# Placing the first feed-forward units' transfers and the modulation columns in a two-layer hybrid trunk

## The chip, the cores and the metric

One core of a Trainium2 chip. The metric is the device time of one execution in microseconds (us); a kernel's time is the median of its runs. Five engines run their own instruction queues in order: TensorE (PE, with its weight loads as PEld), VectorE (DVE), ScalarE (ACT), GpSimd (POOL) and SyncE (SP). SP, ACT and POOL also issue DMA transfers from their queues.

## The reference

Two layers of a decoder trunk over a sequence of 1024 positions with 1024 channels. Each layer has a mixer (scan, pooling and attention side by side, then one output projection) and a gated feed-forward part of width 2816 with a causal convolution of width 3. Both are modulated by a vector that is computed from the condition `c`:

```python
c_act = jax.nn.silu(c)
for i in range(DEPTH):
    mod = (c_act @ ada_w[i] + ada_b[i])[:, None, :]
    sh1, sc1, g1, sh2, sc2, g2 = jnp.split(mod, 6, axis=-1)
    h = rmsnorm(x, norm1_g[i]) * (1.0 + sc1) + sh1
    ...
    x = x + g1 * (mix @ w_out[i])
    h = rmsnorm(x, norm2_g[i]) * (1.0 + sc2) + sh2
    x = x + g2 * conv_ffn(h, ffn_up[i], ffn_conv_w[i], ffn_conv_b[i], ffn_down[i])
return rmsnorm(x, final_g)

def conv_ffn(h, up, conv_w, conv_b, down):
    hid = causal_dwconv(h @ up, conv_w, conv_b)
    g, u = jnp.split(hid, 2, axis=-1)
    return (jax.nn.silu(g) * u) @ down
```

## The kernel before, in words

Activations lie with 128 channels on the partitions and the 1024 positions along the row, so `x` is eight tiles of 128x1024; `H0` and `H1` are the two halves of a row. A 32-bit product is made of three matmuls: both operands are split into a rounded part (`whi`, an ACT cast) and a rest (`wlo`, a DVE subtraction).

**Order.** The program is written as a sequence of tile operations. A scheduler sets the order on each engine: it takes operations by priority (their place in the code) as soon as their tiles and dependencies allow it, so an operation whose inputs are free early is placed far ahead of its line. `after(ins, dep, info)` (line 78) adds a dependency by hand. With `nosync`, the default, it only holds the order; with `sync` the instruction also waits for `dep` on the chip.

**End of the output projection.** The projection has two groups of four input chunks. The second group is `accum_last` (line 1233), called at line 1148. It goes over the first half of the positions for eight output tiles `n`, and then over the second half. Per tile: load the weights through `wraw` (line 265, two raw buffers, issued on SP) and split them, 12 matmuls into a bank `dn`, add into `x[n]` on DVE (`accum`, line 1210), store `x[n]` to memory from ACT's queue (`store`, line 893), square on ACT and add the square into `acc` (`square_add`, line 182: POOL for `n` up to 6, DVE for the last). The weights of tiles 4 to 7 are kept for the second half (`wkeep`). After a half, `rstd_begin` (line 198) sums `acc` over the partitions on PE (`ssps`, L203), ACT and DVE make the scale from it, and `rstd_spread` (line 208) spreads it on PE (L211). Through the second half run `first_half` (line 896), which makes the operands `B` of the first half, and at its end `begin` (line 994), the first seven products of the up projection. `second_half` starts `others` (line 912), which makes the operands T1 to T4 and B22; its subtractions `xx` at L918 run on POOL.

**Up projection.** Pairs of columns are made as 22 units, each with seven products instead of eight, on sums of weight blocks: `S1`, `S2`, `S3`, `S4`, and the plain blocks `A11`, `A12`, `A22`. `prepare` (line 1018) loads the blocks: plain transfers on SP (`up_w`, line 987) and adding transfers on POOL's queue (`plus`): S1 and S3 from memory, then S1 into S2, then S2 into S4. The blocks lie in a ring of sixteen 128x512 buffers. For units 0 and 1 `prepare` is called ahead of `accum_last` (lines 1146 and 1147). Their plain transfers wait for the last accumulation of the first group (`group_last`), and their eight adding transfers are put in the list `pending`. `sums` (line 1010), called per tile, hands them out in the second half; but the scheduler holds no order between them and the tile, so it places them on POOL where their blocks are loaded.

**Modulation columns.** `ada_col` (line 138) makes one column of the modulation: two transfers of 256 KB on SP (`araw`) and two DVE products with a sum. In layer 0's up projection twelve columns are written, one behind each unit from 7 to 18 (`ada`, line 1152). They use the two raw buffers of `wraw`. `finish` (line 1172) does the convolution of a unit, its silu, the product `fg<-fg,fu` on DVE and the store `act_d` on SP.

Of the kernel before, what the change touches and what calls it, by code (L numbers as in the profile page):

```python
# [12 lines left out]
ALU = mybir.AluOpType  # L13
# [41 lines left out]
def tile_trunk(ctx, tc, xT_d, c_d, ck_d, adas_d, pos_d, par_d, pff_d, fg_d, adaw_d, win_d, wv_d, poolw_d, wout_d, up_d, down2_d, down_d,  # L55
               cmask_d, crow_d, out_d):
    nc = tc.nc
# [76 lines left out]
    x = []  # L134
    act.activation(ccol, ccol, AF.Silu)
    act.activation(cact, cact, AF.Silu)

    def ada_col(l, j, take=None):

        for i in range(2):  # L140
            r = take("araw") if take else rawp.tile([128, 528], F32, tag="raw", name="araw")[:, 0:512]
            nc.sync.dma_start(r, adaw_d[l, j, :, HALF[i]])
            dve.scalar_tensor_tensor(r, r, 1.0, cact[:, HALF[i]], ALU.mult, ALU.mult,  # L143
                                     accum_out=mod[l][:, j:j + 1] if i == 0 else mod2[:, j % 8:j % 8 + 1])
        if j % 8 == 7:
            s = slice(j - 7, j + 1)
            dve.tensor_tensor(mod[l][:, s], mod[l][:, s], mod2, op=ALU.add)
            ada_fin(l, j // 8, 0, 8)
# [33 lines left out]
    def square_add(acc, t, first, eng=dve):  # L182
        if first:
            return act.activation(acc, t, AF.Square)
        sq = p2("sq", "nh", 3)[:, 0:acc.shape[-1]]
        r = act.activation(sq, t, AF.Square)
        eng.tensor_tensor(acc, acc, sq, op=ALU.add)  # L187
        return r

    def rstd(acc, n, tab):  # L190
# [20 lines left out]
            spread_last[0] = mm(ps[:, b * 128:(b + 1) * 128], r[:, b:b + 1].to_broadcast([128, 128]), ident, start=True, stop=True)  # L211
        return ps[:, 0:nb * 128]

    spread_last = [None]

    def modulate(l, which, k, hs, rs, hi, lo):
        t = p2("ht", "nh", 3)[:, 0:rs.shape[-1]]
# [651 lines left out]
    def ffn(l, ys, end):  # L869
# [135 lines left out]
                    units[f].V1 = pb("pv", ("ps", "ps", "po")[f])  # L1005
                    product(units[f].V1, raw, "B21", True, spread_last[0] if i == 3 else None, w)

        pending = []

        def sums(part, n):  # L1010

            if part and pending and n < 7:
                pending.pop(0)()
                if n == 6:
                    while pending:
                        pending.pop(0)()

        def prepare(f):

            u = units.setdefault(f, Unit())  # L1020
            dep = group_last[0] if f < 2 else None

            def plus(t, src):
                add = lambda: nc.gpsimd.dma_start(t, src, accum_op=ALU.add)  # L1024
                if f < 2:
                    pending.append(add)
                else:
                    add()

            if f > 3:  # L1030
                u.A11 = up_w("A11", f, 0)
            u.S1 = up_w("S1", NFF + f, 0, dep)
            u.S2 = up_w("S2", f, 0, dep)
            u.S3 = up_w("S3", f, 0, dep)
            plus(u.S1, up_d[l, NFF + f, :, HALF[1]])
            plus(u.S3, up_d[l, NFF + f, :, HALF[0]])
            plus(u.S2, u.S1)
            u.A22 = up_w("A22", NFF + f, 1, dep)
            if f > 2:
                u.A12 = up_w("A12", f, 1)  # L1040
            u.S4 = up_w("S4", f, 1, dep)
            plus(u.S4, u.S2)
# [100 lines left out]

        minus = pff[:, 0:132].rearrange("p (s c) -> p s c", s=3)[:, :, NFF:2 * NFF]
        dve.tensor_scalar(minus, minus, -1.0, None, op0=ALU.mult)
        prepare(0)
        prepare(1)
        accum_last(wout_d[l, 1], ys, 16, l, None, PARTS[0], first_half, begin, second_half, store, sums)

        todo = [(0, 40 + k) for k in range(8)] + [(1, p * 8 + k) for p in (1, 0, 2, 4, 3, 5) for k in range(8)] if l == 0 else []  # L1150

        def ada(n, take=None):
            for _ in range(n):
                if todo:
                    ada_col(*todo.pop(0), take)

        def acts(fs, pool):
            out = []
# [8 lines left out]
            return out  # L1167


        si = None  # L1170

        def finish(f):
            nonlocal si
            p = units.pop(f)
            g = conv(p.G, f, "fg")
            u = conv(p.U, NFF + f, "fu")
            si = act.activation(g, g, AF.Silu)
            dve.tensor_tensor(g, g, u, op=ALU.mult)
            (nc.sync if f < NFF - 2 else nc.gpsimd).dma_start(act_d[f], g)

        for f in range(NFF + 1):
# [26 lines left out]
    cnt_, group_last = [0], [None]  # L1208

    def accum(ps, n, hs, gcol, l):  # L1210
        dve.scalar_tensor_tensor(x[n][:, hs], ps, mod[l][:, gcol + n:gcol + n + 1], x[n][:, hs],
                                 ALU.mult, ALU.add)

    def acc_ps():
# [18 lines left out]
    def accum_last(src, m, gcol, l, dep, parts, then, early, rest=None, store=None, sums=None):  # L1233

        mh, ml = zip(*m)
        tab = table(dep)
        w, done = [], None
        for hs in parts:
            acc = p2("acc", "nr", 2)[:, 0:hs.stop - hs.start]
            for n in range(8):  # L1240
                if not done:
                    w.append(wquad(src, n, True))
                elif early:
                    then(n, *done)
                ps = acc_ps()[:, 0:hs.stop - hs.start]
                gemm(ps, w[n], mh, ml, hs, range(4))
                accum(ps, n, hs, gcol, l)
                if store:
                    store(n, hs)
                square_add(acc, x[n][:, hs], n == 0, nc.gpsimd if rest and n < 7 else dve)  # L1250
                if sums:
                    sums(hs.start, n)
                if done and not early:
                    then(n, *done)
            done = hs, rstd_spread(*rstd_begin(acc, D, "pt", tab))
        if early:
            early()
        if rest:
            rest(*done)
        else:  # L1260
            for n in range(8):
                then(n, *done)
# [134 lines left out]
```

## Time and profile before

| | us |
|---|---|
| median of three runs | 2290.52 |
| lowest and highest | 2285.11, 2291.4 |
| the profiled execution | 2287.57 |
| its span in the trace | 2285.8 |
| granted clock of PE over the span | 0.991 of full speed |

In a profile's row, times are us from the start of the span; L161 is line 161 of the kernel. `dn<-yh,whi` names what is written and what is read, without buffer numbers. What stands in square brackets is the idle time of the engine just before the instruction, and what ended it. In the list of waits the columns are: who waited for whom, us in total, how often, the longest. In a row by windows, each engine has its busy time with the number of instructions in brackets, and the last three numbers are PE's granted clock, the busy share of the DMA engines and GB/s. SPq, ACTq and POOLq are the queues from which an engine issues transfers.

### The profile page before, as it was taken

To read this page: it belongs to the slowest core of one execution; us is meant where nothing else is said; L and a number is where in the kernel's file an instruction comes from. 1 tells how busy PE (TensorE), PEld (TensorE's weight loads), DVE (VectorE), ACT (ScalarE), POOL (GpSimd) and SP (SyncE) were. 2 spreads that over 40 slices of the span, in tenths; PEclk is the share of its full clock that TensorE was granted. 3 is DMA by queue.
4 is the path that set the end of the run, shared out by engine and by line. 5 is a ranking of instruction groups with operands and counts; after the bars stand their busy time and mean duration, and the time that the engine had idled before them with its cause. 6 is when DMAs were issued, how large, how long until landed. Compare 5 with 4: busy or idle time off the path is not lost. (4 is left out here: it accounts for less than half of the span.)

```text
span 2285.8 us, 29760 instructions
## 1 busy us (share of the span) xinstructions
PE 2225.1 (97%) x10472; PEld 1808.7 (79%) x10472; DVE 1553.3 (68%) x2712; ACT 1057.5 (46%) x1960; POOL 243.4 (11%) x308
## 2 busy tenths in 40 slices
PE   6999999999999999999999999998999999999998
PEld 4878877778788888788888888776888888878887
DVE  6467888588766667995564567775966666675446
ACT  5366664355454445312234667533645455442212
POOL 0210000231111110000001000003211111100000
PEclk9999999999999999999999999999999999999999
DMA  7452333658876776991133221236777777663112
GB/s 275 130 146 79 93 112 126 164 161 221 212 197 172 179 175 202 338 298 59 56 134 108 56 56 48 87 106 183 181 179 174 175 175 179 162 244 106 47 47 88
DMA packets 186229, 338.94 MB, mean 148 GB/s; under 512 B 28704, under 2 KB 44320, under 8 KB 186080
## 3 DMA queue, kind: packets, MB, share of 16 engines
q1 hardware_dynamic: 126144, 244.44, 32.8%
q0 software_dynamic: 30560, 61.56, 15.0%
q10 hardware_dynamic: 29376, 31.05, 4.1%
q8 instruction: 82, 1.34, 0.2%
q14 instruction: 67, 0.55, 0.1%
HBM read 265.93 MB, written 44.83 MB: 136 GB/s over the span
## 5 line engine op out<-in xcount | busy, mean ns | idle before, releaser
L161 ACT CAST whi<-wraw 128x512 fp32r<-128x512 f32 (+2 forms) x196 | 117.6, 602 | 394.6 <-PE dq L233 274.1
L232 PE MATMUL dq<-ah,whi 128*128 128x512 f32 x576 | 227.0, 394 | 1.8 <-DVE xd L1230 1.4
L233 PE MATMUL dq<-al,whi 128*128 128x512 f32 x576 | 226.8, 394 | 0.0
L234 PE MATMUL dq<-ah,wlo 128*128 128x512 f32 x576 | 226.0, 393 | 0.0
L161 ACT CAST whi<-S 128x512 fp32r<-128x512 f32 x176 | 108.7, 619 | 206.9 <-PE px L970 129.0
L162 DVE TENSOR_TENSOR wlo<-wraw,whi 128x512 fp32r<-128x512 f32 (+2 forms) x196 | 129.8, 665 | 103.9 <-ACT whi L161 99.2
L1230 DVE SCALAR_TENSOR_TENSOR xd<-dq,mod,xd 128x1024 f32<-128x1024 f32 x80 | 102.7, 1284 | 123.8 <-PE dq L234 123.8
L162 DVE TENSOR_TENSOR wlo<-S,whi 128x512 fp32r<-128x512 f32 x176 | 124.5, 707 | 80.7 <-ACT whi L161 78.5
L143 DVE SCALAR_TENSOR_TENSOR araw<-araw,cact 128x512 f32<-128x512 f32 x160 | 106.1, 689 | 52.2 <-DMA araw<-in_adaw 51.8
L969 PE MATMUL px<-T24h,whi 128*128 128x512 f32 x352 | 138.9, 395 | 2.6 <-ACT s L1046 2.6
L971 PE MATMUL px<-T24h,wlo 128*128 128x512 f32 x352 | 138.3, 393 | 1.9 <-DVE wlo L162 1.9
L970 PE MATMUL px<-T24l,whi 128*128 128x512 f32 x352 | 138.5, 393 | 0.1
L969 PE MATMUL pv<-B,whi 128*128 128x512 f32 x344 | 135.7, 394 | 0.0
L970 PE MATMUL pv<-B,whi 128*128 128x512 f32 x344 | 135.6, 394 | 0.0
L971 PE MATMUL pv<-B,wlo 128*128 128x512 f32 x344 | 135.3, 393 | 0.0
L232 PEld LDWEIGHTS dq<-ah,whi 128*128 128x128 f32 x576 | 108.3, 188 | 28.0 <-issue 1.9
L1137 DVE SCALAR_TENSOR_TENSOR fg<-G,pff,fg 128x1023 f32<-128x1023 f32 x88 | 112.7, 1281 | 24.4 <-ACT fg L1135 24.3
L234 PEld LDWEIGHTS dq<-ah,wlo 128*128 128x128 f32 x576 | 108.4, 188 | 25.0 <-DVE wlo L162 0.5
L161 ACT CAST whi<-A 128x512 fp32r<-128x512 f32 x118 | 72.5, 615 | 118.9 <-PE pv L970 58.0
L233 PEld LDWEIGHTS dq<-al,whi 128*128 128x128 f32 x576 | 108.5, 188 | 23.9
L162 DVE TENSOR_TENSOR wlo<-A,whi 128x512 fp32r<-128x512 f32 x118 | 80.9, 686 | 63.8 <-ACT whi L161 59.5
L1024 POOL DMA_DIRECT2D S<-S x88 | 75.9, 871 | 430.2 <-DMA S<-in_up 284.2
(403 smaller groups left out, 5891.0 us busy)
## 6 DMA issues: line engine op xcount, KB each, us to landing
S<-in_up SPq DMA_DIRECT2D x176, 256.0 KB, 3.0
araw<-in_adaw SPq DMA_DIRECT2D x160, 256.0 KB, 4.2
A<-in_up SPq DMA_DIRECT2D x118, 256.0 KB, 3.6
S<-in_up POOLq DMA_DIRECT2D x88, 256.0 KB, 5.3
S<-S POOLq DMA_DIRECT2D x88, 256.0 KB, 4.0
raw<-act_d SPq DMA_DIRECT2D x88, 256.0 KB, 3.8
act_d<-fg SPq DMA_DIRECT2D x40, 512.0 KB, 3.6
wraw<-in_down SPq DMA_DIRECT2D x80, 256.0 KB, 2.7
```

Of the source, the lines that this page charges most:

```text
L143: dve.scalar_tensor_tensor(r, r, 1.0, cact[:, HALF[i]], ALU.mult, ALU.mult, accum_out=mod[l][:, j:j + 1] if i == 0 else mod2[:, j % 8:j % ...
L161: act.copy(hi[:, 0:n], raw)
L162: dve.tensor_tensor(lo[:, 0:n], raw, hi[:, 0:n].bitcast(F32), op=ALU.subtract)
L232: mm(ps, wh, hi[k][:, s], start=i == 0, stop=False)
L233: mm(ps, wh, lo[k][:, s], start=False, stop=False)
L234: mm(ps, wl, hi[k][:, s], start=False, stop=i == n - 1)
L969: after(mm(ps, wh[:, c], h_, start=first and k == 0, stop=False, skip_group_check=not first), dep)
L970: mm(ps, wh[:, c], l_, start=False, stop=False, skip_group_check=not first)
L971: mm(ps, wl[:, c], h_, start=False, stop=k == 3, skip_group_check=not first)
L1024: add = lambda: nc.gpsimd.dma_start(t, src, accum_op=ALU.add)
L1137: dve.scalar_tensor_tensor(acc[:, s:T], t[:, 0:T - s], pff[:, (2 - s) * 44 + cc:(2 - s) * 44 + cc + 1], acc[:, s:T], ALU.mult, ALU.add)
L1230: group_last[0] = dve.scalar_tensor_tensor(x[n], ps, mod[l][:, gcol + n:gcol + n + 1], x[n], ALU.mult, ALU.add)
```

## The change

Three edits. (1) `prepare` of units 0 and 1 is called from `sums` at tile 6 of the first half, and their plain transfers wait for that tile's accumulation (`row`). (2) Their adding transfers are tied in order to the adds of the squares: S1 and S3 behind tile 2 of the second half, S2 behind tile 4, S4 behind tile 6. (3) In the up projection each column's DVE products stand, in order only, behind the product of the unit finished last (`fg_last`). In the down projection (`take` given) columns have no such dependency.

```diff
-    def ada_col(l, j, take=None):
+    def ada_col(l, j, take=None, dep=None):
...
-            dve.scalar_tensor_tensor(r, r, 1.0, cact[:, HALF[i]], ALU.mult, ALU.mult,
-                                     accum_out=mod[l][:, j:j + 1] if i == 0 else mod2[:, j % 8:j % 8 + 1])
+            after(dve.scalar_tensor_tensor(r, r, 1.0, cact[:, HALF[i]], ALU.mult, ALU.mult,
+                                           accum_out=mod[l][:, j:j + 1] if i == 0 else mod2[:, j % 8:j % 8 + 1]), dep)
...
-        eng.tensor_tensor(acc, acc, sq, op=ALU.add)
+        square_last[0] = eng.tensor_tensor(acc, acc, sq, op=ALU.add)
...
-        pending = []
-
-        def sums(part, n):
-
-            if part and pending and n < 7:
-                pending.pop(0)()
-                if n == 6:
-                    while pending:
-                        pending.pop(0)()
-
-        def prepare(f):
+        def sums(part, n, row, sq):
+
+
+            if not part and n == 6:
+                for f in (0, 1):
+                    prepare(f, row)
+            elif part and n in (2, 4, 6):
+                for f in (0, 1):
+                    for t, src in units[f].sums[{2: slice(0, 2), 4: slice(2, 3), 6: slice(3, 4)}[n]]:
+                        after(nc.gpsimd.dma_start(t, src, accum_op=ALU.add), sq)
+
+        def prepare(f, dep=None):

             u = units.setdefault(f, Unit())
-            dep = group_last[0] if f < 2 else None
+            u.sums = []

             def plus(t, src):
-                add = lambda: nc.gpsimd.dma_start(t, src, accum_op=ALU.add)
                 if f < 2:
-                    pending.append(add)
+                    u.sums.append((t, src))
                 else:
-                    add()
+                    nc.gpsimd.dma_start(t, src, accum_op=ALU.add)
...
-        prepare(0)
-        prepare(1)
...
-                    ada_col(*todo.pop(0), take)
+                    ada_col(*todo.pop(0), take, None if take else fg_last[0])
...
-            dve.tensor_tensor(g, g, u, op=ALU.mult)
+            fg_last[0] = dve.tensor_tensor(g, g, u, op=ALU.mult)
...
-                accum(ps, n, hs, gcol, l)
+                row = accum(ps, n, hs, gcol, l)
...
-                    sums(hs.start, n)
+                    sums(hs.start, n, row, square_last[0])
```

The same edits are made in both layers, except that layer 1 has no columns in its up projection. PE's order stays as it was. What moves on the other engines:

POOL's queue in layer 0's output projection before, from S2 of unit 0 on (S1 and S3 of unit 0 stand ahead of it; `acc_3937` is the first half's sum):

```order
L1024 DMA S2_3918<-S1_3916 128x512
L187 ISA
L187 TENSOR_TENSOR acc_3937<-acc_3937,sq_3981 128x512
L1024 DMA S4_3924<-S2_3918 128x512
L187 TENSOR_TENSOR acc_3937<-acc_3937,sq_4005 128x512
L1024 DMA S1_3926<-in_up 128x512
L187 TENSOR_TENSOR acc_3937<-acc_3937,sq_4029 128x512
L1024 DMA S3_3930<-in_up 128x512
L187 TENSOR_TENSOR acc_3937<-acc_3937,sq_4052 128x512
L187 TENSOR_TENSOR acc_3937<-acc_3937,sq_4075 128x512
L1024 DMA S2_3928<-S1_3926 128x512
L187 TENSOR_TENSOR acc_3937<-acc_3937,sq_4098 128x512
```

The same queue now, where the six adds of the first half and the first of the second (`acc_4141`) stand ahead of the piece:

```order
L187 TENSOR_TENSOR acc_4141<-acc_4141,sq_4203 128x512
L1017 DMA S1_4081<-in_up 128x512
L1017 DMA S3_4085<-in_up 128x512
L1017 DMA S1_4091<-in_up 128x512
L1017 DMA S3_4095<-in_up 128x512
L187 TENSOR_TENSOR acc_4141<-acc_4141,sq_4229 128x512
L187 TENSOR_TENSOR acc_4141<-acc_4141,sq_4251 128x512
L1017 DMA S2_4083<-S1_4081 128x512
L1017 DMA S2_4093<-S1_4091 128x512
L187 TENSOR_TENSOR acc_4141<-acc_4141,sq_4275 128x512
L187 TENSOR_TENSOR acc_4141<-acc_4141,sq_4297 128x512
L1017 DMA S4_4089<-S2_4083 128x512
```

The adding transfers have left the first half and stand between the adds of the second. Behind the piece follow S4 of unit 1, the first adding transfer of unit 2 and then the subtractions `xx` of L918; before, only unit 2's transfer stood between the second half's adds and `xx`.

SP's queue at the same place before (`wraw<-in_wout` are the weights of the output projection's sixteen tiles, S and A the plain transfers of units 0 and 1):

```order
L267 DMA wraw<-in_wout 128x512 x14
L989 DMA S_3916<-in_up 128x512
L989 DMA S_3918<-in_up 128x512
L989 DMA S_3920<-in_up 128x512
L989 DMA A_3922<-in_up 128x512
L989 DMA S_3924<-in_up 128x512
L989 DMA S_3926<-in_up 128x512
L989 DMA S_3928<-in_up 128x512
L989 DMA S_3930<-in_up 128x512
L989 DMA A_3932<-in_up 128x512
L989 DMA S_3934<-in_up 128x512
L267 DMA wraw<-in_wout 128x512 x2
```

And now:

```order
L267 DMA wraw<-in_wout 128x512 x16
L267 DMA wraw<-in_up 128x512 x2
L989 DMA S_4081<-in_up 128x512
L989 DMA S_4083<-in_up 128x512
L989 DMA S_4085<-in_up 128x512
L989 DMA A_4087<-in_up 128x512
L989 DMA S_4089<-in_up 128x512
L989 DMA S_4091<-in_up 128x512
L989 DMA S_4093<-in_up 128x512
L989 DMA S_4095<-in_up 128x512
L989 DMA A_4097<-in_up 128x512
L989 DMA S_4099<-in_up 128x512
```

The last two weight tiles and the first two up tiles now go ahead of the ten plain transfers; the other five up tiles of `begin` follow them.

DVE's queue in layer 0's up projection before, at the eighth column, where the first group of columns is closed (`araw` rows are the columns' products):

```order
L1178 TENSOR_TENSOR fg<-fg,fu 128x1024
L143 SCALAR_TENSOR_TENSOR araw,mod_103<-araw,cact 128x512
L162 TENSOR_TENSOR wlo<-S_5126,whi 128x512
L143 SCALAR_TENSOR_TENSOR araw,mod_101<-araw,cact 128x512
L162 TENSOR_TENSOR wlo<-A_5133,whi 128x512
L143 SCALAR_TENSOR_TENSOR araw,mod_103<-araw,cact 128x512
L162 TENSOR_TENSOR wlo<-S_5122,whi 128x512
L147 TENSOR_TENSOR mod_101<-mod_101,mod_103 128x8
L143 SCALAR_TENSOR_TENSOR araw,mod_102<-araw,cact 128x512
L152 TENSOR_TENSOR mod_101<-mod_101,par_99 128x8
L1051 TENSOR_TENSOR G<-pv,U_5034 128x512
L162 TENSOR_TENSOR wlo<-A_5276,whi 128x512
```

And now, at the same column, nine units further on:

```order
L1176 TENSOR_TENSOR fg<-fg,fu 128x1024
L143 SCALAR_TENSOR_TENSOR araw,mod_101<-araw,cact 128x512
L162 TENSOR_TENSOR wlo<-S_6568,whi 128x512
L143 SCALAR_TENSOR_TENSOR araw,mod_103<-araw,cact 128x512
L147 TENSOR_TENSOR mod_101<-mod_101,mod_103 128x8
L152 TENSOR_TENSOR mod_101<-mod_101,par_99 128x8
L162 TENSOR_TENSOR wlo<-A_6575,whi 128x512
L162 TENSOR_TENSOR wlo<-S_6564,whi 128x512
L1051 TENSOR_TENSOR G<-pv,U_6470 128x512
L162 TENSOR_TENSOR wlo<-A_6725,whi 128x512
```

Up to six products stood in one unit; now each of twelve units has two, right behind its `fg`. On SP a column's two transfers stand behind the store `act_d` of the unit before, and wait for the products of the column before to leave the two raw buffers, so they go out one unit ahead of their own products.

More of the change, by code (lines that the diff above doesn't have):

```diff
@@ L212, in rstd_spread @@
         return ps[:, 0:nb * 128]
-    spread_last = [None]
+    spread_last, square_last = [None], [None]
     def modulate(l, which, k, hs, rs, hi, lo):
@@ L1167, in acts @@
             return out
-        si = None
+        si, fg_last = None, [None]
         def finish(f):
@@ L1210, in accum @@
     def accum(ps, n, hs, gcol, l):
-        dve.scalar_tensor_tensor(x[n][:, hs], ps, mod[l][:, gcol + n:gcol + n + 1], x[n][:, hs],
+        return dve.scalar_tensor_tensor(x[n][:, hs], ps, mod[l][:, gcol + n:gcol + n + 1], x[n][:, hs],
                                  ALU.mult, ALU.add)
```

## The prediction

> **What bounds the kernel now.** I start with the page's first table: TensorE (PE) is busy for almost the whole span, so time can be won only where PE waits or runs at a lower clock. The list of PE's waits over the whole run then names every such place:
>
> ```profile
> PE 2225.1 (97%) x10472; PEld 1808.7 (79%) x10472; DVE 1553.3 (68%) x2712; ACT 1057.5 (46%) x1960; POOL 243.4 (11%) x308
> PE ssps L203 <- DVE acc L187: 11.8, 3, 8.1
> PE dn L232 <- ACT wkeep L261: 4.6, 2, 2.8
> PE px L969 <- ACT s L1046: 2.6, 2, 1.9
> PE px L971 <- DVE wlo L162: 1.9, 1, 1.9
> PE px L970 <- DVE T13l L910: 1.8, 2, 1.4
> ```
>
> The first two rows belong to the last group of the output projection, the others to the up projection: exactly the two places that the change touches. PE's timeline puts them in time. The first and last rows of each layer below are the first matmul of the output projection's last group and the first of the up projection (`px<-B`):
>
> ```profile
> 421.81 0.39 PE L232 MATMUL dn<-yh,whi 128*128 128x512 f32 x1
> 441.41 0.80 PE L232 MATMUL dn<-yh,wkeep 128*128 128x512 f32 x1 [2.80 <-ACT wkeep L261]
> 454.10 1.40 PE L203 MATMUL ssps<-ones,acc 128*128 128x1 f32 x8 [2.10 <-DVE acc L187]
> 478.19 0.40 PE L969 MATMUL px<-B,whi 128*128 128x512 f32 x1
> 1536.35 0.40 PE L232 MATMUL dn<-yh,whi 128*128 128x512 f32 x1
> 1572.40 1.87 PE L203 MATMUL ssps<-ones,acc 128*128 128x1 f32 x8 [8.10 <-DVE acc L187]
> 1595.68 0.39 PE L969 MATMUL px<-B,whi 128*128 128x512 f32 x1
> ```
>
> So the stage takes 478.19 - 421.81 = 56.38 us in layer 0 and 1595.68 - 1536.35 = 59.33 us in layer 1. Why PE waits 8.10 us there stands in the chain of work that ended last, in order of time:
>
> ```profile
> 1559.45 1.47 DMA S<-S
> ...
> 1562.23 4.53 issue
> ...
> 1567.38 1.56 POOL acc L187
> ```
>
> The sum of squares of the first half (`acc`) is built by POOL. In POOL's queue the adding transfers of the first two units stand between those adds, and each waits until an earlier transfer has landed; the 4.53 us "issue" ends when the next adding transfer goes out. Behind POOL come DVE's last add and PE's `ssps`, the row at 1572.40.
>
> **The change part by part.** *1. The output projection.* The ten plain transfers of units 0 and 1 leave the place ahead of the last two weight tiles, and the eight adding transfers leave the first half's POOL queue. What that removes is measured against an undisturbed stage. Its price per matmul, and that of the two small groups at a boundary, come from the second half of layer 0, which has no wait:
>
> ```profile
> 467.08 0.40 PE L232 MATMUL dn<-yh,wkeep 128*128 128x512 f32 x1
> 481.86 0.95 PE L203 MATMUL ssps<-ones,acc 128*128 128x1 f32 x8
> 484.38 1.05 PE L211 MATMUL ssps<-ident,rcol 128*128 128x128 f32 x8
> 455.00:460.00 5.00, 5.00 (x17) 4.23 (x17) 0.80 (x4) 1.10 (x3) 0.86 (x1) 0.50 0.64 157
> ```
>
> From 467.08 to 478.19 run 48 matmuls: 0.2315 us each. A stage has 2 x 8 x 12 = 192 of them and one boundary, 2.0 us by the rows at 481.86 and 484.38: 44.4 + 2.0 = 46.4 us. Layer 0 thus loses 56.4 - 46.4 = 10.0 us, layer 1 59.3 - 46.4 = 12.9 us, **22.9 us together**. Of layer 0's loss 2.80 + 2.10 are waits; the other 5.1 us are matmuls at a low clock after them: the window 455 to 460, behind the second wait, has a granted clock of 0.50 (the number ahead of the last two).
>
> The Trainium skill, page TensorE: Matmul & The Clock Gate, section "Part 1: The HAM clock gate", says that PE falls to half rate after an idle window of about 3.4 us. Here the half clock already follows a wait of 2.10 us, so the trace does not agree with that length; by the page the 5.1 us would have another cause and the sum below would be smaller by them. I keep the trace.
>
> Do both waits go altogether? The weights: the two tiles' transfers were issued at 432.60 and after, behind ten others, and the cast waited for one until 440.74:
>
> ```profile
> 432.60 2.19 SPq L267 DMA_DIRECT2D wraw<-in_wout  x2
> 440.74 0.62 ACT L261 CAST wkeep<-wraw 128x512 fp32r<-128x512 f32 x1 [3.60 <-DMA wraw<-in_wout]
> 1140.20 1.05 PE L203 MATMUL ssps<-ones,acc 128*128 128x1 f32 x8
> ```
>
> Their buffers were free by 432.60 at the latest. A plain load that goes alone lands in 3.6 us (1599.87 to 1603.46, below); with it and the cast's 0.62 the tile would be ready at 436.8, and PE wanted it at 441.41 - 2.80 = 438.6. The sum of squares: the nearest undisturbed boundary is that of layer 0's down projection at 1140.20, where PE has no wait. There DVE makes the adds, here POOL makes six of seven, at 1.30 us each against 2.8 us of PE per tile, so they keep up. I count both waits as gone. What is late next is nothing in that half.
>
> *2. The second half* now carries the load, and this is the cost. Layer 1, counted from the spread of the first half's scale (L211), since nearly all work after it follows from it:
>
> ```profile
> 1577.67 1.05 PE L211 MATMUL ssps<-ident,rcol 128*128 128x128 f32 x8
> 1585.96 1.30 POOL L187 TENSOR_TENSOR acc<-acc,sq 128x512 f32<-128x512 f32 x1 [0.78 <-ACT sq L186]
> 1591.63 1.30 POOL L187 TENSOR_TENSOR acc<-acc,sq 128x512 f32<-128x512 f32 x1 [0.68 <-ACT sq L186]
> 1599.87 0.33 SPq L989 DMA_DIRECT2D S<-in_up  x1
> 1603.46 0.87 POOL L1024 DMA_DIRECT2D S<-in_up  x1 [5.99 <-DMA S<-in_up]
> 1605.69 0.63 ACT L906 ACTIVATE T13h<-xx 128x512 fp32r<-128x512 f32 x1 [2.91 <-POOL xx L918]
> 1606.87 1.83 DVE L162 TENSOR_TENSOR wlo<-S,whi 128x512 fp32r<-128x512 f32 x1 [0.48 <-ACT whi L161]
> 1628.25 0.50 PE L970 MATMUL px<-T13l,whi 128*128 128x512 f32 x1 [0.43 <-DVE T13l L910]
> S<-in_up POOLq DMA_DIRECT2D x88, 256.0 KB, 5.3
> S<-S POOLq DMA_DIRECT2D x88, 256.0 KB, 4.0
> ```
>
> Read from below: PE waits 0.43 us for DVE at 1628.25; DVE has no slack back to 1606.87, where it waits for ACT, which at 1605.69 waited for POOL's subtractions (`xx`, L918). Those stand on POOL behind unit 2's first adding transfer (1603.46, 25.8 us after the spread), which waits for unit 2's plain load, issued at 1599.87. In the built program that load takes the buffer of unit 0's S2 and therefore also waits until S2 has been added into unit 0's S4. That addition was long over; now it is the end of a chain of three. Row 2's add ends at 9.6; S1's addition goes out and lands 5.3 later, 14.9; S2's stands behind row 4's add, which ends at 15.3, and lands 4.0 later, 19.3; S4's stands behind the adds of rows 5 and 6, about 20, and lands at 24; the load, at its own 3.6 us (1603.46 - 1599.87), makes 27.6. That is 1.8 us later than 25.8. Eight additions close together will be slower than the page's medians: between 1559.45 and 1566.78 (the chain above: 1562.23 + 4.53) one took 7.3 us beside plain loads. With 7.3 for each link the result is 9.6 + 3 x 7.3 + 3.6 = 35.1, or 9.3 late. Bounds: 0 (if the load is gated by something else) and 9.3; I take **3 us per layer**, near the medians, because the plain loads are over by then. DVE passes it on to PE in full.
>
> Two smaller costs: the third up tile's load now queues behind the ten plain ones, as the weight tile did that landed 8.1 us after its issue (432.60 to 440.74) instead of 3.6: 0 to 4.5 us late, I take 0.7, near 0, because its buffer comes free only after the boundary, when most of the ten have landed. And POOL's adds of rows 5 and 6 stand behind S2's second addition, 0 to 1, I take 0.3. Together 4 us per layer, **8 us**. POOL's eight issues are hidden in its own idle time. On SP only five up tiles and the next unit's loads stand behind the new wait for row 6; PE needs these later, apart from the one counted.
>
> *3. The modulation columns.* Twelve columns (24 transfers, 24 DVE products) move from the start of layer 0's up projection to one per unit. What they cost where they stood, and where they will stand:
>
> ```profile
> 588.74 0.69 DVE L143 SCALAR_TENSOR_TENSOR araw<-araw,cact 128x512 f32<-128x512 f32 x1 [5.92 <-DMA araw<-in_adaw]
> 591.64 1.24 ACT L1135 ACTIVATE fg<-G,pff 128x1024 f32<-128x1024 f32 x1 [6.43 <-DVE G L1051]
> 598.27 0.51 PE L971 MATMUL px<-T24h,wlo 128*128 128x512 f32 x1 [1.91 <-DVE wlo L162]
> 643.34 0.69 DVE L162 TENSOR_TENSOR wlo<-A,whi 128x512 fp32r<-128x512 f32 x1 [2.11 <-ACT whi L161]
> ```
>
> DVE waits 5.92 us for a column's transfer, ACT then 6.43 us for DVE, and PE at 598.27 for DVE's next weight split. The first list's rows for `s` (2.6) and `wlo` (1.9) are this and two more between 598 and 624 us, all in layer 0, where the columns are. They go: 4.5 us. One product of 0.69 us also stood in the DVE stretch before T13, where PE waits 1.4 us in layer 0: 0.7 us more. At the new place, behind the unit's product, DVE waits 2.11 us for ACT anyway (643.34, a unit without columns), room for 2 x 0.69 us; the transfer goes out a unit ahead, as the order shows, so DVE need not wait for it. SP is held behind `act_d` until both products are done, a few us per unit. I take **5.2 us gained**, bounds 0 and 6.
>
> Sum: 22.9 + 5.2 - 8 = 20.1 us. The profiled run took 2287.57 us (span 2285.8), so **2267.5**; the three runs' median is 2.95 above it, their lowest 2.46 below it, so it stands between them and I leave the number as it is.
>
> **The rivals.**
> - *All of it is hidden* (costs of 2 at their lower bounds): 2287.6 - 28.1 = 2259.5. For it: the additions in the up projection land in 4 to 5 us. Against: the chain of three starts only after row 2.
> - *The wait moves to the second half*: each link takes 7.3 us as in the chain shown, 9.3 + 1 per layer: 28.1 - 20.6 = 7.5 gained, 2280.
> - *The columns disturb the units*: if each of the twelve made PE wait 1.5 us (4.5 us over the three waits of today), 18 us: about 2285.5. Against it speaks DVE's idle time at 643.34.
> - *Slower.* The same POOL chain decides it, through the length of one link. With a link of t the subtractions come 9.6 + 3t + 3.6 - 25.8 = 3t - 12.6 us late per layer; two layers eat 28.1 us from t = 8.9 on. The longest landing of any `S` transfer is 10.6:
>
> ```profile
> DMA to landing us min/median/max: 2.4/3.9/10.6
> ```
>
>   With that in every link it is 19.2 us per layer, and 2287.6 - 28.1 + 38.4 = 2298. The median of 3.9 speaks against it.
> - That nothing moves is excluded by the order rows.
>
> **How the numbers follow.** Forecast 0.60 (2267.5), all hidden 0.15 (2259.5), moved wait 0.15 (2280), disturbed units 0.05 (2285.5), slower 0.05 (2298). A range from 2257 to 2281 takes in the first three. A measurement of this kernel tells about 0.3% (6.9 us of the median of 2290.5) from no change, so "faster" is below 2283.6: 0.90; the disturbed units are "same", 0.05; slower 0.05.
>
> **What would show it.** Right: in the changed profile PE waits neither for `wkeep` nor, at the first half's `ssps`, for `acc`; the granted clock stays at 1.00 through both stages; each stage up to the first `px<-B` takes 46 to 48 us; DVE has no wait for `araw` in the units; `xx` (L918) starts 28 to 30 us after the first spread and PE's wait for T13 or T24 in each layer is 2 to 4 us. Wrong: a wait at `ssps` in either half above 2 us, `xx` more than 35 us after the spread, or waits of PE for `wlo` spread over the twelve units.

## The result, and the profile after

The changed kernel takes 2274.62 us, median of 4 runs (2273.75 to 2276.22); the kernel before 2290.2 (2285.11 to 2291.4). The ratio is 0.9934, with a 95% interval of 0.9915 to 0.9953. The profiled execution took 2274.38 us (span 2272.6), 13.2 us less than that of before. The time lies inside the range, 7 us above the forecast.

The list of PE's waits over the whole run has lost the rows for `wkeep`, `s` and `wlo`. The row for `acc` is still there:

```profile
PE ssps L203 <- DVE acc L187: 8.7, 3, 3.8
PE px L970 <- DVE T13l L910: 2.8, 2, 1.4
```

The third `ssps` of the first row is that of the end of the run. PE's timeline puts the others in time. For layer 0 it shows the first matmul of the stage, the first half's boundary (`ssps` and the spread), the first matmul of the up projection, the second half's `ssps`, the first matmul with T24 and the wait at T13; then rows of layer 1, and the last spread of the run:

```profile
421.05 0.39 PE L232 MATMUL dn<-yh,whi 128*128 128x512 f32 x1
446.45 0.95 PE L203 MATMUL ssps<-ones,acc 128*128 128x1 f32 x8
449.19 1.05 PE L211 MATMUL ssps<-ident,rcol 128*128 128x128 f32 x8
467.23 0.40 PE L969 MATMUL px<-B,whi 128*128 128x512 f32 x1
474.27 1.84 PE L203 MATMUL ssps<-ones,acc 128*128 128x1 f32 x8 [3.21 <-DVE acc L187]
494.56 0.39 PE L969 MATMUL px<-T24h,whi 128*128 128x512 f32 x1
508.10 0.50 PE L970 MATMUL px<-T13l,whi 128*128 128x512 f32 x1 [1.37 <-DVE T13l L910]
1528.12 0.40 PE L232 MATMUL dn<-yh,whi 128*128 128x512 f32 x1
1574.18 0.39 PE L969 MATMUL px<-B,whi 128*128 128x512 f32 x1
1581.89 1.35 PE L203 MATMUL ssps<-ones,acc 128*128 128x1 f32 x8 [3.82 <-DVE acc L187]
1615.24 0.50 PE L970 MATMUL px<-T13l,whi 128*128 128x512 f32 x1 [1.38 <-DVE T13l L910]
2264.87 1.05 PE L211 MATMUL ssps<-ident,rcol 128*128 128x128 f32 x4 [1.25 <-DVE rcol L180]
```

The wait for `acc` has changed its place: the first half's boundary (446.45) has none, the second half's has 3.21 and 3.82 us. Two windows of layer 0 show what follows it (the granted clock is the number ahead of the last two):

```profile
470.00:475.00 5.00, 1.79 (x9) 1.30 (x7) 4.73 (x6) 1.45 (x4) 3.93 (x4) 0.81 1.04 257
475.00:480.00 5.00, 5.00 (x18) 4.32 (x18) 1.18 (x4) 1.55 (x4) 0.00 (x0) 0.51 0.80 153
```

| stretch of PE, us | before L0, L1 | after L0, L1 | difference |
|---|---|---|---|
| first `dn` to first `px<-B` | 56.38, 59.33 | 46.18, 46.06 | -23.5 |
| first `px<-B` to first T24 | 21.27, 21.35 | 27.33, 28.52 | +13.2 |
| first T24 to the wait at T13 | 12.49, 11.22 | 13.54, 12.54 | +2.4 |
| layer 0, that wait to its down projection | 402.67 | 397.37 | -5.3 |

These four make -13.2, as much as the difference of the profiled executions; what lies outside them differs by less than 1 us in each part and cancels. So the stage gains what it should, and the second boundary gives half of that back. VectorE (DVE) shows why. Its queue in layer 0's second half, from the spread on, with duration as the second column (`acc` is its last add of squares):

```profile
450.27 1.40 DVE L898 SCALAR_TENSOR_TENSOR xx<-xx,acol,ssps 128x512 f32<-128x512 f32 x2 [1.67 <-PE ssps L211]
...
455.11 0.69 DVE L162 TENSOR_TENSOR wlo<-wraw,whi 128x512 fp32r<-128x512 f32 x1 [0.84 <-ACT whi L161]
...
462.72 1.57 DVE L902 SCALAR_TENSOR_TENSOR B<-xx,mod,B 128x512 fp32r<-128x512 f32 x1
...
465.52 1.81 DVE L902 SCALAR_TENSOR_TENSOR B<-xx,mod,B 128x512 fp32r<-128x512 f32 x1
...
469.24 2.01 DVE L910 TENSOR_TENSOR wkeep<-wraw,wkeep 128x512 fp32r<-128x512 f32 x1
471.17 0.74 DVE L1209 SCALAR_TENSOR_TENSOR xx<-dn,mod,xx 128x512 f32<-128x512 f32 x1
...
473.45 0.68 DVE L187 TENSOR_TENSOR acc<-acc,sq 128x512 f32<-128x512 f32 x1
```

DVE is idle once (0.84 us, for the third up tile) between 450.27 and 474.13: this **chain** takes 23.86 us, in layer 1 24.40. Before it took 20.74 and 20.47, and ended here:

```profile
480.93 0.68 DVE L187 TENSOR_TENSOR acc<-acc,sq 128x512 f32<-128x512 f32 x1
```

PE's `ssps` followed at 481.86, 0.25 us later. So DVE reached this boundary together with PE already, and had no slack, though PE showed no wait. Now some of L902 and L910 take 1.6 to 2.0 us in place of 0.7. POOL's queue at that time:

```profile
460.21 3.54 POOL L1017 DMA_DIRECT2D S<-in_up  x4
462.45 4.34 POOL L187 TENSOR_TENSOR acc<-acc,sq 128x512 f32<-128x512 f32 x2
466.73 0.85 POOL L1017 DMA_DIRECT2D S<-S  x1
468.52 0.85 POOL L1017 DMA_DIRECT2D S<-S  x1 [0.93 <-DMA S<-in_up]
469.08 3.29 POOL L187 TENSOR_TENSOR acc<-acc,sq 128x512 f32<-128x512 f32 x2
...
482.09 0.85 POOL L1028 DMA_DIRECT2D S<-in_up  x1 [7.12 <-DVE wlo L162]
482.65 5.34 POOL L918 TENSOR_TENSOR xx<-xx 128x512 f32<-128x512 f32 x4
```

The long DVE instructions lie beside POOL's adds, which four issues at 460.21 and two more have pushed out of step. L902 and L910 read two operands from SBUF; L898 and L1209, which read one from PSUM, keep their 0.74.

**Port theory:** a DVE instruction with two SBUF operands and an add of POOL take turns; the issues between the adds bring them together. **Issue theory:** the issuing itself holds DVE up. **Queue theory:** POOL's last adds come late behind the transfers, and DVE's `acc` waits for them. **Load theory:** the plain transfers make the up tiles late. Beside these, unit 2's first adding transfer (482.09) still stands ahead of `xx`: the **gate** of the prediction. It waits for unit 2's plain load, which went out at 478.46, and SP had waited 4.5 us for an `S<-S` transfer to land (the second row is from the list of SP's waits between 470 and 500):

```profile
478.46 0.33 SPq L989 DMA_DIRECT2D S<-in_up  x1
SPq L989 <- DMA S<-S: 5.0, 2, 4.5
```

### The profile page after: what moved, and what is told of

It is laid out like the page before. It is cut to its first block, busy times and chain, and to the rows that moved or that the text cites. A ratio compares the mean times of both kernels' runs of the same rounds, so it can differ in the third digit from the quotient of the medians.

```text
span 2272.6 us, 29749 instructions
## 1 busy us (share of the span) xinstructions
PE 2220.7 (98%) x10472; PEld 1804.1 (79%) x10472; DVE 1559.5 (69%) x2712; ACT 1059.3 (47%) x1960; POOL 244.4 (11%) x308
## 4 chain that ended last, share of the span: by engine, by line
PE 86%; DVE 6%; DMA 4%; issue 1%; ACT 1%; POOL 0%; ACTq 0%; SPq 0%; DVEq 0%; POOLq 0%
PE px L970 7%; PE px L969 7%; PE px L971 7%; PE dq L232 6%; PE dq L233 6%; PE dq L234 6%; PE pv L970 5%; PE pv L969 5%; PE pv L971 5%; PE dn L234 2%; PE dn L233 2%; PE dn L232 2%; DMA araw<-in_adaw 2%; PE qk L232 1%; PE qk L233 1%
## 5 line engine op out<-in xcount | busy, mean ns | idle before, releaser
L233 PEld LDWEIGHTS dq<-al,whi 128*128 128x128 f32 x576 | 108.3, 188 | 23.9
L1137 DVE SCALAR_TENSOR_TENSOR fu<-U,pff,fu 128x1023 f32<-128x1023 f32 x88 | 112.3, 1276 | 0.1
```

Of the source, the lines that this page charges most:

```text
L233: mm(ps, wh, lo[k][:, s], start=False, stop=False)
L1137: dve.scalar_tensor_tensor(acc[:, s:T], t[:, 0:T - s], pff[:, (2 - s) * 44 + cc:(2 - s) * 44 + cc + 1], acc[:, s:T], ALU.mult, ALU.add)
```

## The experiments

e1 is a small program of its own and e5 is made from the kernel before; the others are the changed kernel with the edits shown (e8, e10 and e11 build on e7). The stretch ahead of the first `dn` is the same code in all; in the profiled executions it ends between 421 and 428 us. So beside the times stands, for each profiled execution, the time from its first `dn` to the last spread (1856.1 before, by 421.81 and 2277.87; 1843.8 after). The chain is DVE's, from the first L898 to the end of the last add of squares.

| run | median, us | ratio to before (95%) | `dn` to end | DVE's chain L0, L1 | wait at second `ssps` |
|---|---|---|---|---|---|
| before | 2290.2 | | 1856.1 | 20.7, 20.5 | 0, 0 |
| changed | 2274.62 | 0.9934 (0.9915 to 0.9953) | 1843.8 | 23.9, 24.4 | 3.2, 3.8 |
| e2_noadd | 2266.09 | 0.9888 (0.9875 to 0.9902) | 1829.7 | 20.6, 21.2 | 0, 0.6 |
| e3_nosq | 2272.42 | 0.9920 (0.9905 to 0.9935) | 1838.9 | 19.8, 19.6 | 0, 0 |
| e4_early | 2279.43 | 0.9952 (0.9939 to 0.9964) | 1848.7 | 25.5, 25.3 | 1.4, 0.8 |
| e5_cols | 2287.57 | 0.9975 (0.9965 to 0.9985) | 1851.7 | 20.5, 20.5 | 0, 0 |
| e6_xfer | 2282.45 | 0.9952 (0.9938 to 0.9965) | 1846.0 | 23.9, 24.4 | 3.3, 3.8 |
| e7_ahead | 2276.98 | 0.9921 (0.9908 to 0.9934) | 1838.5 | 21.9, 21.6 | 1.2, 1.1 |
| e8_ahead2 | 2266.94 | 0.9882 (0.9867 to 0.9896) | 1833.9 | 21.9, 22.8 | 1.2, 1.3 |
| e9_xxfirst | 2271.91 | 0.9906 (0.9885 to 0.9926) | 1838.4 | 23.7, 23.4 | 3.0, 2.8 |
| e10_ahead3 | 2263.40 | 0.9873 (0.9849 to 0.9896) | 1831.1 | 21.8, 22.3 | 1.0, 0.9 |
| e11_ahead4 | 2264.64 | 0.9873 (0.9856 to 0.9891) | 1832.9 | 21.1, 21.4 | 0.7, 0.9 |

The kernel before, run beside them, had medians of 2291.33 (e2 to e4), 2293.91 (e5 to e8) and 2296.24 (e9 to e11); so runs of different sets are compared by their ratios.

### The disputed cost by itself

In e1 `two` counts DVE instructions with two SBUF operands, `one` those with one operand in PSUM, `adds` POOL's adds and `issues` its adding transfers.

```diff
+    phase(0, two=8)
+    phase(1, one=8)
+    phase(2, adds=8)
+    phase(3, one=8, adds=5)
+    phase(4, two=8, adds=5)
+    phase(5, two=12, issues=6)
+    phase(6, one=12, issues=6)
```

> A small program in place of the kernel; nothing of the reference is computed. VectorE runs rows of 128x512 instructions: first alone with two SBUF operands, then alone with one operand in PSUM; POOL runs eight 128x512 adds alone; then each of the two VectorE forms beside five POOL adds, and each beside six adding transfers that POOL issues. Port theory: alone 0.67 to 0.74 us for VectorE and 1.30 us for POOL. Beside POOL's adds the form with two SBUF operands takes turns with them: the mean of one rises by 0.5 us or more and some take 1.5 to 2.0 us; the form with a PSUM operand stays at its 0.74. Beside the issues both forms stay. Issue theory: beside the issues one or both forms rise to 1 us or more, beside the adds neither does.

Groups of e1 by phase, the phases in this order: two SBUF operands alone; one in PSUM alone; the second and then the first beside POOL's adds; two SBUF operands beside issues. The row with x2 is the stretch from 40.5 to 42.5 us, in the middle of the fourth of these phases. The number behind the busy time is the mean of one in ns:

```profile
L83 DVE SCALAR_TENSOR_TENSOR two<-two,s 128x512 f32<-128x512 f32 x7 | 4.8, 692 | 0.2
L87 DVE SCALAR_TENSOR_TENSOR one<-ps,one 128x512 f32<-128x512 f32 x7 | 4.8, 691 | 0.2
...
L91 POOL TENSOR_TENSOR sum<-sum,q 128x512 f32<-128x512 f32 x4 | 5.1, 1266 | 0.3
L87 DVE SCALAR_TENSOR_TENSOR one<-ps,one 128x512 f32<-128x512 f32 x7 | 4.8, 691 | 0.2
...
L83 DVE SCALAR_TENSOR_TENSOR two<-two,s 128x512 f32<-128x512 f32 x7 | 9.6, 1364 | 0.2
L83 DVE SCALAR_TENSOR_TENSOR two<-two,s 128x512 f32<-128x512 f32 x2 | 3.3, 1634 | 0.1
L91 POOL TENSOR_TENSOR sum<-sum,q 128x512 f32<-128x512 f32 x4 | 6.4, 1590 | 0.3
...
L83 DVE SCALAR_TENSOR_TENSOR two<-two,s 128x512 f32<-128x512 f32 x11 | 7.6, 692 | 0.4
```

With two SBUF operands an instruction goes from 692 to 1634 ns beside POOL's adds. The mean of 1364 is lower because POOL had finished before the last two of the seven, which took 692 again. POOL's add goes from 1261 alone to 1590. With one operand in PSUM neither changes (691, and 1266 for POOL), and issues change nothing. The port theory holds, the issue theory falls. The Trainium skill, page SBUF — State Buffer, section "Who interferes with whom", says that a DVE instruction with two SBUF inputs contends with a GpSimd instruction that reads SBUF; this run agrees. One instruction of each together take 1.67 us here (the time from one DVE instruction to the next), a little less than the 0.69 + 1.26 us of the two alone.

### One side of the meeting left out

e2 leaves out the eight adding transfers with their issues, e3 the adds:

```diff
-            elif part and n in (2, 4, 6):
+            elif part and n in ():
```

> The changed kernel without the eight adding transfers of units 0 and 1 in each layer (their sums of blocks are left out); POOL's adds of squares in the second half and the ten plain transfers stay. In the changed kernel VectorE needs 23.9 (layer 0) and 24.4 us (layer 1) from the first L898 to the end of its last add of squares, and 20.7 and 20.5 before the change. Port theory (POOL's adds, shifted by the issues between them, meet VectorE's instructions with two SBUF operands) and queue theory (POOL's last adds come late behind the transfers): 20.5 to 21.8 us, PE's two waits at the second ssps fall from 3.2 and 3.8 to 0 to 1.5 us, and the clock after it stays at 1.00: 2262 to 2268 us. Load theory (the ten plain transfers make the up tiles late): 23 us or more, waits of 2.5 us or more, 2272 to 2276.

```diff
-        square_last[0] = eng.tensor_tensor(acc, acc, sq, op=ALU.add)
+        square_last[0] = r if skip else eng.tensor_tensor(acc, acc, sq, op=ALU.add)
...
-                        after(nc.gpsimd.dma_start(t, src, accum_op=ALU.add), sq)
+                        after(nc.gpsimd.dma_start(t, src, accum_op=ALU.add), sq, sync)
...
-                square_add(acc, x[n][:, hs], n == 0, nc.gpsimd if rest and n < 7 else dve)
+                square_add(acc, x[n][:, hs], n == 0, nc.gpsimd if rest and n < 7 else dve,
+                           sums and done and 0 < n < 7)
```

> The changed kernel without POOL's six adds of squares in the second half of the output projection in each layer (left out of the sum); the eight adding transfers go out behind the squares of the same tiles. Port theory: no VectorE instruction of L902 or L910 takes over 1.15 us there, 20.5 to 21.8 us from the first L898 to the last add of squares, waits at the second ssps of 0 to 1.5 us, 2263 to 2269 us. Issue theory (the issuing itself holds VectorE up): the instructions of 1.5 to 2.0 us remain, waits of 2.5 us or more, 2272 to 2276. Queue theory: VectorE's long instructions remain, the waits are gone all the same.

In e2 the adds keep step, the chain is close to that before the change (20.6 and 21.2) and the waits are nearly gone (0 and 0.6): 14.1 us less than the changed kernel (1843.8 - 1829.7). That is the whole price of the eight transfers. POOL's and DVE's last adds in layer 0 of e2:

```profile
471.68 1.89 POOL L187 TENSOR_TENSOR acc<-acc,sq 128x512 f32<-128x512 f32 x1 [0.69 <-ACT sq L186]
474.65 0.68 DVE L187 TENSOR_TENSOR acc<-acc,sq 128x512 f32<-128x512 f32 x1
```

In e3 no instruction of DVE's chain is long any more (none above 0.8), though the issues are there: again port, not issue. But it came out at 2272.42, above its 2263 to 2269: the waits at `ssps` are gone and others stand behind them:

```profile
476.13 0.62 ACT L909 CAST wkeep<-wraw 128x512 fp32r<-128x512 f32 x1 [2.12 <-DMA wraw<-in_up]
...
478.07 1.16 PE L211 MATMUL ssps<-ident,rcol 128*128 128x128 f32 x8 [2.33 <-DVE rcol L180]
...
1598.04 0.51 PE L969 MATMUL px<-T24h,whi 128*128 128x512 f32 x1 [2.14 <-ACT s L1046]
```

The last up tile landed late, and its cast stands ahead of `rcol` on ACT; in layer 1 `xx` came 31.3 us after the first spread (26.4 before). The queue theory isn't needed: in the changed kernel POOL's adds end at 469.08 + 3.29 = 472.37, ahead of DVE's `acc` at 473.45, and DVE is not idle ahead of that. That last add stands behind the square of the last tile, which waits for L1209 at 471.17, held by the 2.01 us ahead of it.

### The issues at another place

```diff
-            elif part and n in (2, 4, 6):
+            elif part and n in (0, 2, 6):
...
-                    for t, src in units[f].sums[{2: slice(0, 2), 4: slice(2, 3), 6: slice(3, 4)}[n]]:
+                    for t, src in units[f].sums[{0: slice(0, 2), 2: slice(2, 3), 6: slice(3, 4)}[n]]:
```

> The changed kernel with S1 and S3 of units 0 and 1 issued ahead of POOL's first add of squares of the second half, where POOL is idle for 11.8 us, S2 behind the second of these adds and S4 behind the sixth. Only two issues (S2) then stand between the adds. Port theory: two or three of VectorE's long instructions go, 21 to 22.5 us instead of 23.9 and 24.4, the waits at the second ssps fall to 0.5 to 2.0 us, 2266 to 2271 us. Queue theory: the waits are gone, since the rows 5 and 6 stand behind no transfer: 2264 to 2267. Load theory: unchanged, 2273 to 2276.

The time was missed by every theory: 2279.43, above the changed kernel. The waits at the second `ssps`, 1.4 and 0.8 us, are as the port theory said, and the long instructions go (one of 1.88 and 1.86 is left per layer, as in the kernel before), but the third up tile is late. Its cast on ACT, a wait of PE behind it, and the window in which it was under way (DMA share ahead of the last number):

```profile
463.35 0.62 ACT L161 CAST whi<-wraw 128x512 fp32r<-128x512 f32 x1 [6.10 <-DMA wraw<-in_up]
466.07 0.50 PE L232 MATMUL dn<-yh,wkeep 128*128 128x512 f32 x1 [2.23 <-DVE xx L1209]
455.00:460.00 5.00, 5.00 (x23) 4.02 (x22) 3.99 (x6) 1.93 (x3) 0.76 (x1) 1.00 1.09 286
```

The four additions go out while the ten plain transfers are still under way, and DVE is idle 4.9 us for that tile. So the load theory is true of this place, not of the changed kernel, where that idle time is 0.84 and 0.70. e7 therefore moves the plain transfers as well, and then all issues out of the adds:

```diff
-            if not part and n == 6:
+            if not part and n == 3:
...
+            elif part and n in (0, 6):
+                for k in ((slice(0, 2), slice(2, 3)) if n == 0 else (slice(3, 4),)):
```

> The changed kernel with the ten plain transfers tied to tile 3 of the first half instead of tile 6, S1, S3 and S2 issued in POOL's idle time ahead of the second half's adds, and S4 behind the sixth add: no issue stands between the adds any more, and the plain transfers are over before the third up tile is loaded. Port theory: VectorE's chain takes 20.5 to 21.5 us (23.9 and 24.4 in the changed kernel), the waits at the second ssps are 0 to 1 us, and only xx, held by unit 2's transfer until S4 has landed, is late: 2264 to 2269 us. Transfer theory (so many transfers in so short a time are what slows the stage, wherever they stand): up tiles or kept weights come late instead, PE waits for dn or px in all 3 us or more per layer, 2272 or more.

The chain is 21.9 and 21.6, the waits 1.2 and 1.1; from first `px<-B` to first T24 PE needs 24.3 and 24.2 us (27.3 and 28.5 in the changed kernel). This gives back 3.0 + 4.3 = 7.4 us. e3, without the adds, gives back 6.1 of the same stretch (25.4 and 24.4 us). So the port's part is some 6 to 7 us; neither run isolates it, since the loads of the up tiles come at other times too. In e7 DVE is still idle 1.3 and 1.8 us for them, and the chain and the waits lie just above the expected 21.5 and 1 us. `xx` is still 4.2 and 4.5 us behind the second spread, and PE waits 1.38 us at T13 in each layer. By the trace it is 5.3 us under the changed kernel; by the times the two can't be told apart (0.9921 beside 0.9934), and 2276.98 is not the 2264 to 2269 expected. That time is in the range of the transfer theory, but PE's waits for `px` are 1.7 and 1.4 us per layer, not the 3 that it asked for. The five runs lie 6.7 us apart, which no row explains.

### The gate

```diff
-                    nc.gpsimd.tensor_tensor(x[k][:, H0], t, x[k][:, H0], op=ALU.subtract)
+                    xx_last[0] = nc.gpsimd.tensor_tensor(x[k][:, H0], t, x[k][:, H0], op=ALU.subtract)
...
-                    nc.gpsimd.dma_start(t, src, accum_op=ALU.add)
+                    after(nc.gpsimd.dma_start(t, src, accum_op=ALU.add), xx_last[0] if f == 2 else None)
```

e9 does this to the changed kernel, e8 to e7.

> The changed kernel with unit 2's first adding transfer behind the four subtractions xx on POOL, and nothing else. Gate theory (in the changed kernel unit 2's transfer, held until S4 of unit 0 has landed, holds up xx): xx starts 2.1 to 2.8 us after the second spread (3.55 now), PE's waits at T13 of 1.37 and 1.38 us fall to 0.5 or less, the waits at the second ssps stay at 3 to 4 us; 2 to 5 us less than the changed kernel, a ratio to the kernel before of 0.991 to 0.9925 (0.9934 now). If xx is held by VectorE alone: no change, 0.993 to 0.994.

> As the kernel before it, with unit 2's first adding transfer put behind the four subtractions xx on POOL. If unit 2's transfer holds up xx and so T13: xx starts 2.1 us after the second spread in place of 3.5 or more, PE's waits at T13 fall by 0.5 to 1.5 us per layer, 1 to 3 us less than the kernel before it. If unit 2's sums are the tighter end: PE waits in unit 2 instead, no gain or up to 3 us more.

In e9 `xx` starts 2.7 and 2.0 us after the second spread, and the waits stand about as expected, the boundary's still there (3.0 and 2.8 us), those at T13 nearly gone:

```profile
474.84 1.84 PE L203 MATMUL ssps<-ones,acc 128*128 128x1 f32 x8 [3.02 <-DVE acc L187]
506.69 0.50 PE L970 MATMUL px<-T13l,whi 128*128 128x512 f32 x1 [0.33 <-DVE T13l L910]
```

It is 5.5 us under the changed kernel by the trace (1843.8 - 1838.4), 2.7 us per layer; the intervals of the two ratios overlap. Between the first T24 and the wait at T13 the layers gain 2.4 and 1.4 us. Most of the rest lies ahead of T24 in layer 1, where DVE's chain was 1.0 us shorter; that the edit caused this is not shown. In e8 PE's waits at T13 are 0.2 us or less; by the trace it is 4.6 us under e7, more than the 1 to 3 expected, and by the ratios 9 (0.9882 beside 0.9921). The profiled execution of e7 was 4.1 us under its median and that of e8 4.4 above; what the other runs of e7 have on top stays open.

### The edits apart

e5 is the kernel before with the third edit alone, e6 the changed kernel without it:

```diff
-                    ada_col(*todo.pop(0), take, None if take else fg_last[0])
+                    ada_col(*todo.pop(0), take)
```

> The kernel before with the third edit alone (each column's products behind the product of the unit finished last); the output projection stays as it was before. If the edits add up: PE's three waits of 4.5 us between 598 and 624 us go, and with the matmuls at a lower clock behind them about 5.3 us: 2284 to 2287 us, and the waits for wkeep and for the first half's acc are there as before. If the gain of the columns in the changed kernel came from the other edits: 2289 to 2292.

> The changed kernel without the third edit (the columns are placed as before). If the edits add up: 2274.6 + 5.3, 2279 to 2281 us, with PE's waits for s and wlo between 590 and 625 us and the waits at the second ssps of 3.2 and 3.8 us. If the columns' products, placed early, also load VectorE in the second half: the waits at the second ssps or at T13 in layer 0 grow by over 1 us, 2282 or more.

By the ratios, e5 gains 0.25% and e6 0.48%, together 0.73%, and both at once gave 0.66%: they add up within their intervals. In ratios, both are as expected for edits that add up. e5's waits for `s` and `wlo` are gone, e6's are there (1.94 and 1.01 us), and e6's second boundary is that of the changed kernel.

### A faster version

e10 and e11 are e8 with one and two of DVE's L910 instructions (the rests of kept up tiles) behind its last add of squares (e10 is shown; e11 has `i in (4, 5)`):

```diff
-                    hl(*w, raw)
+                    hl(*w, raw, dep=square_last[0] if i == 5 else None)
```

> The fastest kernel so far (plain transfers earlier, no issue between POOL's adds, unit 2 behind xx) with one of VectorE's instructions moved: the rest (wlo part) of the second kept up tile is made behind the last add of squares instead of ahead of it; PE needs it 11 us later. If VectorE's queue alone sets the second ssps: its waits of 1.23 and 1.31 us fall by 0.6 each, 1 to 3 us less, a ratio of 0.987 to 0.988 (0.9882 without it). If something else ends there (ACT's cast, the last up tile's load): no change.

> The same with the rests of the first and the second kept up tile behind the last add of squares. VectorE reaches that add 1.3 us earlier, so the waits at the second ssps would be 0 to 0.3 us, ratio 0.986 to 0.988; but the last up tile's load waits for the buffer that the first rest frees, so it may come late: then PE waits 1 us or more for wkeep or at the second spread, ratio 0.989 or more.

Both reach 0.9873, and can't be told from e8 or from each other; all three are faster than the changed kernel, whose interval begins at 0.9915. The waits fell by 0.3 to 0.5 us only, less than either expectation, so VectorE's queue alone no longer sets the second `ssps`. In e11 its chain has 2.3 and 2.6 us of idle time, for ACT's casts of up tiles, and ACT in turn waits 1.5 to 2.0 us for the load of each of these tiles. The kernel before has no such idle time in the chain, so the loads are the next place to look.

## Why the prediction was right, and where it was not

**1. The output projection: right.** 22.9 us forecast, 23.5 measured; the stage takes 46.2 and 46.1 us, neither wait of the first half is left, and its clock is 1.00. The eight transfers cost nothing there any more: e2's stage is 46.2 and 46.1, too.

**2. The second half: right place, a term too small.** 8 us were forecast; the table above has 13.2 + 2.4 = 15.6, and leaving out the transfers gives 14.1 back. The difference of 7.6 is the 7 us by which the time was missed. Of its three terms:

- The gate, 3 us per layer: 1.9 (T24 to T13 alone) to 2.7 by e9. Its mechanism held: unit 2's load waits for an `S<-S` transfer. It went out 29.3 us after the first spread (24 forecast) and landed 3.6 us later, as forecast. `xx` came 33.5 us after the first spread, later than the 28 to 30 forecast, but the second spread was late by then too, so that `xx` was only 1.4 us later behind that. PE's wait at T13, forecast at 2 to 4 us, was 1.37 and 1.38.
- The third up tile, 0.7: DVE's idle time for it is 0.84 and 0.70. In e2, which has the plain loads and not the eight transfers, the stretch from first `px<-B` to first T24 is 0.2 and 0.8 us longer than before.
- "POOL's adds of rows 5 and 6 stand behind S2's second addition, 0 to 1, I take 0.3": **this step failed.** It looked at when POOL is done, and POOL is done in time. What the later adds do is to meet DVE's L902 and L910: the chain grows by 3.1 and 3.9 us, of which only 0.8 and 0.7 are the up tile. The price was some 3 to 3.7 us per layer (6.1 by e3 and 7.4 by e7 for both).

How the rest of e2's 14.1 us divides between the port, the gate and later up tiles is not measured.

That so little DVE time costs so much is a second oversight in the same part: the forecast took the second boundary as PE's, because PE had no wait there. DVE's chain ended 0.25 us ahead of it (0.17 in layer 1), so whatever lengthens the chain is a wait of PE, and the low clock behind the wait (0.51) comes on top. And the sign was in a row that the prediction quotes: the `wlo` at 1606.87 took 1.83 us beside POOL's subtractions, where its like take 0.69. Only its wait was read.

The rival "the wait moves to the second half" named the place and not the mechanism: it asked for links of 7.3 us. The measured 2274.62 is nearer to its 2280 than to the forecast, and lies in the range because the range was drawn to take this rival in. The sign set for "wrong", a wait above 2 us at an `ssps`, came true.

**3. The columns: right.** 5.2 forecast; 5.3 in the table, and 5.7 by e5 (0.25% of 2293.91). The stretch of the table takes 397.35 us in e5 and 401.35 in e6, so the third edit is worth 5.3 on the kernel before and 4.0 on the changed one. None of the twelve units shows a wait of PE of 0.3 us or more.

**4. The slower rival** needed links of 8.9 us and was far: the whole price was 7 to 8 us per layer, not 14.

## What to carry to other kernels

A boundary at which TensorE does not wait may still be another engine's: compare the end of each engine's chain there before counting on a gain ahead of it. When work is moved between another engine's instructions, ask not only when that engine is done, but which instructions of a busy neighbour it will now meet; an instruction that takes twice the time of its like in the trace is the sign. And move transfers into an engine's idle time together with the loads that they need, or the loads of others pay.

## What the runs showed of the hardware

- DVE with two SBUF operands beside POOL's adds: from 692 to 1634 ns each; with one operand in PSUM 691 and 691 (e1). Four issues in a row occupy POOL for 3.54 us (changed kernel); six beside DVE leave its instructions at 692 ns (e1).
- The clock falls after waits far below the 2.10 us of the profile before. In e11 the two layers are a pair: behind the wait of 0.69 us the clock stays, behind that of 0.91 us it is 0.63 for the next 4 us:

```profile
473.09 1.02 PE L203 MATMUL ssps<-ones,acc 128*128 128x1 f32 x8 [0.69 <-DVE acc L187]
476.00:480.00 4.00, 4.00 (x23) 3.40 (x22) 2.77 (x4) 1.75 (x3) 1.28 (x1) 1.00 0.84 257
1575.26 1.02 PE L203 MATMUL ssps<-ones,acc 128*128 128x1 f32 x8 [0.91 <-DVE acc L187]
1578.00:1582.00 4.00, 4.00 (x17) 3.49 (x17) 1.44 (x2) 0.77 (x2) 0.24 (x1) 0.63 0.66 208
```

  In e10 it fell to 0.68 behind a wait of 0.96 us and stayed at 1.00 behind one of 0.90. So near 0.9 us something else decides as well; which, no run shows. The Trainium skill, page TensorE: Matmul & The Clock Gate, section "Part 1: The HAM clock gate", describes a free-running window of about 3.4 us and ties the fall to an idle window of that length. That length does not fit these rows; whether the phase of the window decides here, no run shows.
- The same code ahead of the first `dn` took 421 to 428 us in twelve profiled executions, as much as half of the change's effect.
